# Partial sums seeded into accumulator banks by ScalarE, and the second norm's modulation made wholly by dot products on VectorE

## The chip, the cores and the metric

The kernel runs on one core of a Trainium2 chip. A core has four compute engines, each with its own queue that is worked off in order: TensorE (PE in the profile; its weight loads are a row of their own, PEld), VectorE (DVE), ScalarE (ACT) and GpSimd (POOL). SyncE (SP) issues most DMA transfers. The metric is the device time of one execution in microseconds (us), the median of several runs.

## The reference

One layer of a diffusion backbone runs over two groups of 128 tokens, the prompt (s = 0) and the sample (s = 1), with the same float32 weights and D = 2048. Cut to what matters here:

```python
m = jax.nn.silu(cvec) @ w_ada + b_ada               # per group: shift1, scale1, gate1, shift2, scale2, gate2
h = rms_norm(x, norm1_w) * (1 + sc1) + sh1
p = h @ w_in                                        # q, k, v of two mixers and two gates: 8704 columns
oa, ob = attention of mixer A and of mixer B        # QK-norm, softmax, 8 heads each
y = (sigmoid(ga) * (oa @ w_br_a) + sigmoid(gb) * (ob @ w_br_b)) @ w_out
x = x + g1 * y
h2 = rms_norm(x, norm2_w) * (1 + sc2) + sh2
x = x + g2 * (square(relu(h2 @ w_up)) @ w_down)     # 2048 -> 8192 -> 2048
```

The outputs are both groups' x and the keys and values of the prompt.

## The kernel before, in words

**Steps.** Every weight comes in tiles of 128 x 1024 float32 (512 KB): two blocks of 128 rows by 512 columns. One such tile is a *step*, numbered through the whole kernel (456 of them, the list `wsteps`). For a step the tile is loaded by SP (`add_step`, line 215), ScalarE rounds it to a high part `wH` (`copy`, line 93) and VectorE subtracts to get the low part `wL` (line 241). Then TensorE makes 12 matmuls: two row blocks, two token groups, and three products each (high x high, low weight x high, high x low activation; `mm3`, lines 291 to 293). An accumulator is one bank of 128 x 512 float32; eight banks exist, four in the pool `pacc` for accumulators and four in `paux`.

**The order by hand.** `run` goes through the steps and emits, for each: the loads that are due (lead `LOAD` plus the digit of `RUN`), the splits up to a look-ahead (the digit of `LOOK`), its matmuls, and then whatever was hung on that step with `at`, `ex` or `load_at`. All constants at the top of the file (`LOOK`, `RUN`, `DOTS`, `POST`, `JOBS` and so on) are such places. For the steps in `LO_DMA` the low part is not made on VectorE: ScalarE writes the negated high part (line 247) and a DMA on the POOL queue adds the weight to it (line 248).

**Stages by step.** Steps 0 to 71 are nine units of the first projection (q, k, v), in five chunks of row blocks (`CHUNKS`: 2, 2, 2, 4 and 6, so 1, 1, 1, 2 and 3 steps a unit), because `h` becomes ready block by block. After its chunk a unit's two banks are copied out by ScalarE (first chunk, `first_evac`) or added to what is in SBUF by VectorE (line 400). Steps 72 to 135 are the gates, with the attention among them (`qk_stat`, `qk_apply`, `att_job`); 136 to 167 the two branch projections; 168 to 199 `w_out` and the second norm; then `w_up` and `w_down` in eight pieces of two 512-column blocks. From the second piece on, some tiles of `w_up` go through a Strassen form (`up_pair`, `FAST`): tiles `tH`, `uH`, `YB`, `XL` are made by VectorE and ScalarE, and seven products replace eight. After each piece come four `down_unit`s. Their partial sums over the pieces are kept in SBUF, `dsum`: the first is copied, the others are added by VectorE (line 1257) or copied and then added by a DMA of the POOL queue (`SUM_DMA`, line 1261). `gate_sum` (lines 1238, 1239) multiplies by the gate and adds to x before the last piece, whose units are added by `resid`.

**The modulation.** silu(c) @ w_ada is made in two ways. On TensorE, by column blocks of 128 (`pair_load`, `pair_mm`, line 308: 32 matmuls a block for shift and scale, from four loads of 512 KB), then a copy by ScalarE, transposes on TensorE (`ada_cols`, line 326) and a few small operations on VectorE. Or on VectorE as *dots*: a transposed weight tile of 128 x 1024 (`dot_load`, 512 KB) times the condition row, broadcast to all partitions (`cB`), with the sum taken along the columns (line 1327). One job is one block, one part and one half of the 2048 rows; it needs one dot for each group. The two gates go as dots entirely; of the second norm's 16 blocks the first 6 (`FB_DVE`) go through TensorE, the other 10 as dots; of the first norm's 16 blocks 14 go through TensorE. The condition row is loaded for each of five runs of jobs, and SiLU is applied each time (`silu_cond`, lines 1309, 1310).

Of the kernel before, what the change touches and what calls it, by code (L numbers as in the profile page):

```python
# [10 lines left out]
F32 = mybir.dt.float32  # L11
# [21 lines left out]
FB_DVE = 6  # L33
FB1 = 14
H_AT = 41
DOTS1 = [11, 17, 20, 28, 28, 31, 34, 37]
CHUNKS = [2, 2, 2, 4, 6]
NFAST = 8
FAST = {1: (0, 3, 7), 2: (0, 2, 6, 7), 3: (0, 2, 4, 5, 7), 4: (0, 2, 4, 5, 7), 5: (0, 3, 4, 5, 7), 6: (0, 2, 4, 5, 7), 7: (0, 1, 2, 4, 5, 7)}
SUM_DMA = [5, 6, 11, 13, 16, 19, 21, 23, 25, 27]  # L40
AWAY = [('gA', 1), ('gB', 2), ('gB', 3), ('gA', 0), ('gB', 0), ('gA', 2)]
GATE_BACK = 8
DIRECT = (3,)
LO_DMA = [70, 83, 107, 131, 176, 184, 233, 292, 314, 328, 402, 404]
LO_AHEAD = 2

LOOK = "443323444122344433223333332123333453344534333554455544344534333543324554444555556665556644444333333333332222122312344544555434333333342344333334333323445566643344456656533344434444445455564546555553444554322355444554433333333434334533333333333654544332334455543444555653215536544523333334543233333332223323365455455443222212233432443334434642333334444544534434333333333325434222223333434444444434555642255353443444442222432331122132223342112223332233345544"
RUN = "301110000000010212223333322222222221111122244455544355434445554334554445555664543433234334444445665543321222222212444444444444442222222232223344444455544544444444555455454445566644455555554543365434343355445756644443566664333312222234552332223333334545332333333333322211122222332233322212233323323332332112344444442343322211333343334323233334544422742222212223445554422333233322222211222333333435767545333110221112232111233456655566567556433435335553333334"
CONST_AT = [65, 67]
XL_DMA = []  # L50
ADA_AT = [None, 4, 13, 18, 21, 36, 29]
XS_AT = {1: 13, 2: 18, 3: 29}
POST = {('kvA', 0): [67, 70, 75], ('qA', 0): [70, 73, 78], ('qA', 1): [72, 74, 80], ('kB', 0): [77, 83, 90], ('qB', 0): [82, 84, 93], ('kB', 1): [86, 91, 93], ('qB', 1): [90, 93, 97]}
JOBS = [[79, 80, 80, 87, 93], [81, 83, 88, 90, 93], [87, 87, 89, 90, 99], [93, 93, 96, 99, 102], [96, 97, 100, 105, 112], [102, 103, 107, 112, 123], [105, 107, 111, 118, 123], [112, 115, 118, 121, 123]]
SS_AT = [43, 51, 73, 75, 139, 139]
T_AT = [4, 4]
PREP_IN = [6, 7]
DOTS = [33, 39, 42, 43, 47, 47, 48, 49, 52, 54, 55, 57, 60, 62, 69, 70, 73, 77, 80, 84, 90, 91, 92, 92, 94, 98, 101, 103, 103, 105, 108, 110, 111, 112, 115, 118, 120, 121, 122, 122, 126, 127, 128, 129, 130, 132, 132, 136, 137, 138, 138, 143, 144, 147, 147, 150, 153, 155, 157, 161, 164, 167, 170, 172, 173, 174, 175, 176, 177, 178, 179, 182]
DOTS2 = [230, 232, 234, 235, 236, 237, 240, 243, 255, 263, 265, 269, 270, 288, 301, 301, 307, 328, 328, 331, 333, 334, 358, 360, 361, 363, 366, 368, 391, 391, 395, 399]
STAT_AT = [-1, 0, 10, 16]  # L60
T_PAIR = [[8, 9], [6, 8], [8, 9], [7, 8], [10, 11], [8, 9], [12, 11]]
P_PAIR = [[4, 2], [2, 4], [3, 4], [1, 3], [6, 6], [3, 3], [6, 5]]
M_TE = (3,)
M_AT = [1, 3, 9]
FLIP = 1
P_UP = [4, 1]
# [5 lines left out]
def tile_hybrid_step(ctx: ExitStack, tc: tile.TileContext, a):  # L72
# [13 lines left out]
    def SM(n, name):  # L86
        return sp.tile([P, 32], F32, name=name, tag="s", bufs=14)[:, :n]
# [195 lines left out]
    def mm3(acc, stat, st, first, last, order=(0, 1)):  # L283

        wh, wl = st["hl"]
        for k in range(2):
            kk = 2 * st["half"] + k
            for tb in order:
                sh, sl = stat(kk, tb)
                f, l = first and k == 0, last and k == 1  # L290
                pe.matmul(acc[tb], sh, wh[:, k, :], start=f, stop=False)  # L291
                pe.matmul(acc[tb], sh, wl[:, k, :], start=False, stop=False)  # L292
                pe.matmul(acc[tb], sl, wh[:, k, :], start=False, stop=l)  # L293
# [77 lines left out]

    def first_evac(u, acc):
        units[u] = G(f"u_{u[0]}{u[1]}").rearrange("p (s n) -> p s n", s=2)
        for tb in range(2):
            copy(units[u][:, tb, :], acc[tb])

    def start_steps(u, k0, nk):

        box = {}

        def mm(st, kt):
            if kt == 0:
                box["acc"] = [bank("acc", pacc) for _ in range(2)]
            acc = box["acc"]
            wh, wl = st["hl"]
            last = kt + 2 == nk
            for k in range(2):
                g, kg = divmod(k0 + kt + k, 4)
                for tb in range(2):
                    sh, sl = hH[g][:, kg, tb, :], hL[g][:, kg, tb, :]  # L390
                    pe.matmul(acc[tb], sh, wh[:, k, :], start=kt == 0 and k == 0, stop=False)  # L391
                    pe.matmul(acc[tb], sh, wl[:, k, :], start=False, stop=False)  # L392
                    pe.matmul(acc[tb], sl, wh[:, k, :], start=False, stop=last and k == 1)  # L393
            if not last:
                return
            if k0 == 0:
                first_evac(u, acc)
                return
            for tb in range(2):
                dve.tensor_tensor(units[u][:, tb, :], units[u][:, tb, :], acc[tb], op=OP.add)  # L400
            box.clear()

        for kt in range(0, nk, 2):
# [1094 lines left out]
```

## Time and profile before

| | |
|---|---|
| median of three runs | 1333.61 us |
| the three runs | 1331.23, 1333.61, 1334.71 us |
| span of the profiled execution | 1331.3 us |
| TensorE busy | 1316.0 us, 99% |
| VectorE busy | 1190.2 us, 89% |
| ScalarE busy | 800.8 us, 60% |
| moved by DMA | 392.24 MB, mean 295 GB/s |

The profiled execution has no time of its own beside its span; the three runs lie from 0.1 us below that span to 3.4 us above. "L291" is line 291 of the kernel. In a group line stand the line, the engine, the operation, the tiles written and read, their shapes and the count; after the first bar the busy time of all and the mean of one in ns; after the second the idle time in front of them and what ended it. In a timeline line stand the start and the duration in us and, in brackets, the idle time before and its releaser. In a table by stretches each engine's busy time stands with its number of instructions in brackets. Ends of matmuls are modelled, so starts are what to go by.

### The profile page before, as it was taken

What the parts mean: (1) busy time and instruction counts of PE and PEld (TensorE: products, weight loads), DVE (VectorE), ACT (ScalarE), POOL (GpSimd) and SP (SyncE); (2) the same over time, 40 slices, a digit from 0 to 9 for tenths busy, and PEclk for the clock granted to TensorE, in tenths of its full rate; (3) what the DMA queues carried; (4) which work ended last, traced back from release to release, by engine and by line L of the source; (5) the groups of instructions that cost most, each with busy time, mean ns of one, the idle gap of its engine ahead of it and who ended that gap; (6) DMA issues with size and microseconds to landing.
All of it is one profiled execution on the core that took longest, in us unless ns stands there. A gap on an engine that the chain in (4) does not pass through costs nothing.

```text
span 1331.3 us, 18039 instructions
## 1 busy us (share of the span) xinstructions
PE 1316.0 (99%) x6411; PEld 1067.0 (80%) x6412; DVE 1190.2 (89%) x1546; ACT 800.8 (60%) x979; POOL 54.6 (4%) x64
## 2 busy tenths in 40 slices
PE   8999999999999999999999999999999999999998
PEld 4777778788888878888888888888888888877887
DVE  4699999988898999999779998998999999989685
ACT  5534443476656446635677866758577576676660
POOL 0000000521000000000000000000000000000000
PEclk9999999999999999999999999999999999999999
DMA  9999998986589999996578876988798696878962
GB/s 374 409 409 408 409 401 300 384 277 240 177 329 355 381 392 356 354 367 214 191 230 280 281 254 215 291 273 266 235 296 255 237 301 206 311 195 291 331 213 98
DMA packets 148267, 392.24 MB, mean 295 GB/s; under 512 B 51793, under 2 KB 53009, under 8 KB 148177
## 3 DMA queue, kind: packets, MB, share of 16 engines
q1 hardware_dynamic: 144448, 378.16, 78.8%
q0 software_dynamic: 3584, 12.85, 5.0%
q8 instruction: 50, 0.82, 0.3%
q14 instruction: 41, 0.33, 0.1%
q10 hardware_dynamic: 144, 0.08, 0.0%
HBM read 367.16 MB, written 8.68 MB: 282 GB/s over the span
## 4 chain that ended last, share of the span: by engine, by line
PE 92%; DMA 4%; DVE 2%; ACT 1%; issue 1%; SPq 0%; DVEq 0%; ACTq 0%
PE acc L291 16%; PE acc L292 16%; PE acc L293 16%; PE Q L1117 6%; PE Q L1119 6%; PE Q L1118 6%; PE acc L391 4%; PE acc L392 4%; PE acc L393 4%; DMA araw<-in_w_pair 3%; PE ps_ada L308 2%; PE ps_S L707 1%; PE Z L1119 1%; PE Z L1117 1%; PE Z L1118 1%; DMA aT<-in_w_adaT 1%
## 5 line engine op out<-in xcount | busy, mean ns | idle before, releaser
L241 DVE TENSOR_TENSOR wL<-raw,wH 128x1024 fp32r<-128x1024 f32 x375 | 446.6, 1225 | 72.0 <-ACT wH L93 67.9
L93 ACT ACTIVATE wH<-raw 128x1024 fp32r<-128x1024 f32 (+1 forms) x393 | 392.8, 1044 | 128.3 <-PE acc L392 23.3
L391 PE MATMUL acc<-wH,hH 128*128 128x512 f32 x276 | 109.1, 395 | 0.0
L393 PE MATMUL acc<-wH,hL 128*128 128x512 f32 x276 | 107.5, 390 | 0.0
L392 PE MATMUL acc<-wL,hH 128*128 128x512 f32 x276 | 107.5, 389 | 0.0
L291 PE MATMUL acc<-wH,hH 128*128 128x512 f32 x256 | 101.4, 396 | 0.0
L293 PE MATMUL acc<-wH,hL 128*128 128x512 f32 x256 | 99.7, 390 | 0.0
L292 PE MATMUL acc<-wL,hH 128*128 128x512 f32 x256 | 99.7, 390 | 0.0
L1327 DVE CUSTOM_DVE_ANT_0 aT<-aT,cB,cols 128x1024 f32<-128x1024 f32 x56 | 71.7, 1286 | 0.2
L1327 DVE CUSTOM_DVE_ANT_0 junk<-aT,cB,cols 128x1024 bf16<-128x1024 f32 x56 | 71.4, 1280 | 0.0
L93 ACT ACTIVATE tH<-t 128x1024 fp32r<-128x1024 f32 x33 | 35.0, 1061 | 58.0 <-DVE t L1172 55.4
L391 PEld LDWEIGHTS acc<-wH,hH 128*128 128x128 f32 x276 | 51.8, 188 | 13.6 <-issue 2.5
L393 PEld LDWEIGHTS acc<-wH,hL 128*128 128x128 f32 x276 | 51.8, 188 | 11.0
L392 PEld LDWEIGHTS acc<-wL,hH 128*128 128x128 f32 x276 | 51.8, 188 | 10.4
L293 PEld LDWEIGHTS acc<-wH,hL 128*128 128x128 f32 x256 | 48.0, 188 | 10.2
L291 PEld LDWEIGHTS acc<-wH,hH 128*128 128x128 f32 x256 | 48.1, 188 | 9.8 <-ACT sq L622 0.4
L292 PEld LDWEIGHTS acc<-wL,hH 128*128 128x128 f32 x256 | 48.1, 188 | 9.4
L93 ACT ACTIVATE uH<-raw 128x1024 fp32r<-128x1024 f32 x33 | 35.1, 1063 | 31.6 <-DVE raw L1177 28.6
L1223 ACT ACTIVATE up<-up 128x1024 f32<-128x1024 f32 x28 | 29.7, 1062 | 26.8 <-DVE up L1217 26.3
L308 PE MATMUL ps_ada<-araw,cpad 128*32 128x256 f32 x640 | 39.1, 382 | 2.7 <-DMA araw<-in_w_pair 2.5
L93 ACT ACTIVATE fTa<-pTa 128x2048 uint16<-128x2048 uint16 x16 | 40.5, 2533 | 2.0 <-PE acc L292 1.4
L1172 DVE TENSOR_TENSOR t<-raw 128x1024 f32<-128x1024 f32 x33 | 40.2, 1219 | 1.0 <-PE acc L292 1.0
(641 smaller groups left out, 3316.7 us busy)
## 6 DMA issues: line engine op xcount, KB each, us to landing
raw<-in_w_in SPq DMA_DIRECT2D x133, 512.0 KB, 9.5
raw<-in_w_down SPq DMA_DIRECT2D x128, 512.0 KB, 5.6
araw<-in_w_pair SPq DMA_DIRECT2D x80, 512.0 KB, 10.2
raw<-in_w_upF SPq DMA_DIRECT2D x66, 512.0 KB, 5.2
aT<-in_w_gT SPq DMA_DIRECT2D x64, 512.0 KB, 6.9
raw<-in_w_up SPq DMA_DIRECT2D x62, 512.0 KB, 5.0
aT<-in_w_adaT SPq DMA_DIRECT2D x48, 512.0 KB, 9.6
raw<-in_w_out SPq DMA_DIRECT2D x32, 512.0 KB, 9.6
```

The costliest lines, as they stand in the source:

```text
L93: act.activation(out, in_, AF.Copy)
L241: dve.tensor_tensor(st["lo"], st["raw"], st["hi"].bitcast(F32), op=OP.subtract)
L291: pe.matmul(acc[tb], sh, wh[:, k, :], start=f, stop=False)
L292: pe.matmul(acc[tb], sh, wl[:, k, :], start=False, stop=False)
L293: pe.matmul(acc[tb], sl, wh[:, k, :], start=False, stop=l)
L391: pe.matmul(acc[tb], sh, wh[:, k, :], start=kt == 0 and k == 0, stop=False)
L392: pe.matmul(acc[tb], sh, wl[:, k, :], start=False, stop=False)
L393: pe.matmul(acc[tb], sl, wh[:, k, :], start=False, stop=last and k == 1)
L1117: pe.matmul(acc, stat[0], hi, start=f, stop=False)
L1118: pe.matmul(acc, stat[0], lo, start=False, stop=False)
L1119: pe.matmul(acc, stat[1], hi, start=False, stop=l)
L1327: dve.tensor_tensor_reduce(out, box["raw"], cB[s, tag], 1.0, dst if second else baT[:, part, fb:fb + 1], OP.mult, OP.add, dst)
```

## The change

- `FB_DVE` is 0: all 16 blocks of the second norm's shift and scale are dots (24 jobs more), and no column block of it goes through TensorE any more.
- A dot is a `scalar_tensor_tensor` (times 1.0, times the row) with `accum_out`, where a `tensor_tensor_reduce` stood. It gives a plain sum; the second half of the rows goes to a small tile of its own, and `dot_sum` adds the halves and the bias once.
- SiLU is applied to each half of the condition row once and written to DRAM by the POOL queue; later runs load the result.
- First projection: where `SEED1` has a 1, ScalarE copies the partial sum from SBUF into the two banks (`seed`, two steps ahead), the chunk's matmuls add to it, and ScalarE copies the result out. The last two units of a chunk keep their banks and are the first two of the next (`KEEP`; the order of units alternates). Two unit-chunks keep the addition on VectorE.
- Last stage: the same for `dsum` (`seed` three steps ahead, or at the end of a Strassen pair). The DMA sums, line 1257 and `gate_sum` go; the last piece's banks hold the whole sum.
- `qk_stat` takes its sums of squares on ScalarE, head by head, with `accum_out`; the softmax division becomes four scaled copies on ScalarE.
- `LO_DMA` has 22 steps, where it had 12; 18 of them, where it had 6, lie before step 200. The Strassen tiles of a pair stand at other positions, as many as before. `LOOK`, `RUN` and the other places are set anew.

```diff
-FB_DVE = 6
+FB_DVE = 0
-SUM_DMA = [5, 6, 11, 13, 16, 19, 21, 23, 25, 27]
+SEED_AT = 3
+KEEP = True
+SEED1_AT = 2
+SEED1 = "011111011101111111111110111111111111"
-LO_DMA = [70, 83, 107, 131, 176, 184, 233, 292, 314, 328, 402, 404]
+LO_DMA = [70, 85, 107, 119, 130, 132, 134, 139, 140, 143, 154, 163, 176, 183, 184, 187, 189, 195, 233, 258, 292, 393]
-SS_AT = [43, 51, 73, 75, 139, 139]
+SS_AT = []
...
+        def seed():
+            seeds1[u] = banks()
+            for tb in range(2):
+                copy(seeds1[u][tb], units[u][:, tb, :])
...
-                    pe.matmul(acc[tb], sh, wh[:, k, :], start=kt == 0 and k == 0, stop=False)
+                    pe.matmul(acc[tb], sh, wh[:, k, :], start=opened[u] and k == 0, stop=False, skip_group_check=skip)
...
+        if seeded:
+            at(i - SEED1_AT, seed)
...
+    turned = first_units[7:] + first_units[2:7] + first_units[:2]
...
         for s in range(2):
-            act.activation(sq[:, s].rearrange("p h d -> p (h d)"), raw[:, s, 0:nh * HD], AF.Square)
-        ssq, r = SM(2 * nh, "ssq"), SM(2 * nh, "rq")
-        dve.tensor_reduce(ssq.rearrange("p (s h) -> p s h", s=2), sq, axis=AX.X, op=OP.add)
+            for h in range(nh):
+                act.activation(sq[:, s, h, :], raw[:, s, h * HD:h * HD + HD], AF.Square,
+                               accum_out=ssq[:, s * nh + h:s * nh + h + 1])
...
-            dve.tensor_tensor(prob[:, :, 0:nk], prob[:, :, 0:nk], rd.unsqueeze(2).to_broadcast([P, 4, nk]), op=OP.mult)
+            for h in range(4):
+                act.activation(prob[:, h, 0:nk], prob[:, h, 0:nk], AF.Copy, scale=rd[:, h:h + 1])
...
+    def seed(p, n):
+
+        seeds[p, n] = [bank("acc", pacc) for _ in range(2)]
         for s in range(2):
-            dve.tensor_tensor(d[:, s, :], d[:, s, :], gbc["g2", n][:, s, :], op=OP.mult)
-            dve.tensor_tensor(x1[n][:, s, :], x1[n][:, s, :], d[:, s, :], op=OP.add)
+            copy(seeds[p, n][s], dsum[n][:, s, :])
...
             for s in range(2):
-                if p == last:
-                    out_s(acc, n, s)
-                elif p == 0 or by_pool:
-                    copy(part[:, s, :], acc[s])
-                else:
-                    dve.tensor_tensor(dsum[n][:, s, :], dsum[n][:, s, :], acc[s], op=OP.add)
...
-                pool.dma_start(dsum[n], part, accum_op=OP.add)
+                copy(dsum[n][:, s, :], acc[s])
...
+        if p and (n or p == last):
+            at(len(wsteps) - SEED_AT, lambda: seed(p, n))
...
-    def silu_cond(s, tag):
+    def silu_cond(h, s, tag):
+        if (s, h) in silu_row:
+            return
         t, c = G("sgB"), cB[s, tag]
         act.activation(t, c, AF.Sigmoid)
         dve.tensor_tensor(c, c, t, op=OP.mult)
+        silu_row[s, h] = dp.tile([1, 1024], F32, name=f"silu{s}{h}")
+        pool.dma_start(silu_row[s, h], c[0:1, :])
...
-        dve.tensor_tensor_reduce(out, box["raw"], cB[s, tag], 1.0, dst if second else baT[:, part, fb:fb + 1],
-                                 OP.mult, OP.add, dst)
+        dve.scalar_tensor_tensor(out, box["raw"], 1.0, cB[s, tag], op0=OP.mult, op1=OP.mult,
+                                 accum_out=dst[:, s, fb:fb + 1])
+
+    def dot_sum(dst, which, part, f0=0):
+        n = KC - f0
+        dve.tensor_tensor(dst, dst, half2.pop(which)[:, :, f0:KC], op=OP.add)
+        dve.tensor_tensor(dst, dst, baT[:, part, f0:KC].unsqueeze(1).to_broadcast([P, 2, n]), op=OP.add)
```

214 lines of the change are left out of this document (127 added, 87 removed).

## The prediction

> **What bounds the kernel now.** First the page: busy time, the slices, the chain that ended last.
>
> ```profile
> PE 1316.0 (99%) x6411; PEld 1067.0 (80%) x6412; DVE 1190.2 (89%) x1546; ACT 800.8 (60%) x979; POOL 54.6 (4%) x64
> ...
> PE   8999999999999999999999999999999999999998
> ...
> DVE  4699999988898999999779998998999999989685
> ACT  5534443476656446635677866758577576676660
> ...
> DMA  9999998986589999996578876988798696878962
> ...
> PE 92%; DMA 4%; DVE 2%; ACT 1%; issue 1%; SPq 0%; DVEq 0%; ACTq 0%
> ```
>
> TensorE is busy in every slice and holds 92% of the chain; VectorE (DVE) stands at 8 or 9 tenths beside it, ScalarE (ACT) at 3 to 7. A busy TensorE row can hide gaps, so next the timeline of a quiet stretch, to see whether matmuls really follow each other:
>
> ```profile
> 599.72 0.39 PE L291 MATMUL acc<-wH,m0H 128*128 128x512 f32 x1
> ...
> 602.44 0.39 PE L291 MATMUL acc<-wH,m0H 128*128 128x512 f32 x1
> ```
>
> Between these two lie 12 matmuls, one weight step: 2.72 us a step, 0.227 a matmul. The change leaves the number of 512-column matmuls as it is (the Strassen positions move, but their number, 33, stays), so time can go only where TensorE does other work or waits. The last place to look is the one long wait in the later half, in the timeline and the table by stretches (columns: TensorE, weight load, VectorE, ScalarE, GpSimd, clock, DMA share, GB/s):
>
> ```profile
> 1195.58 0.39 PE L1119 MATMUL Q<-YB,h20L 128*128 128x512 f32 x1
> 1199.57 0.80 PE L1117 MATMUL Q<-tH,sH 128*128 128x512 f32 x1 [3.60 <-ACT dsum L93]
> ```
> ```profile
> 1195.00:1205.00 10.00, 6.40 (x22) 4.87 (x21) 9.86 (x12) 6.04 (x8) 0.87 (x1) 0.83 0.91 270
> ```
>
> TensorE stood 3.6 us at the head of the last Strassen pair and then ran at a granted clock of 0.83 over the ten us: about 5.3 us lost in all (3.6, and 0.17 of the 10). VectorE was busy 9.86 of these 10: it was late, not idle.
>
> **The change, part by part. (1) The modulation as dots.** FB_DVE goes from 6 to 0, so the six column blocks that TensorE made for the second norm (line 308) go, with their three gathers and transposes (line 326). From the chain in order of time, and the timeline:
>
> ```profile
> 170.45 1.86 PE ps_ada L308 x32
> 194.30 1.86 PE ps_ada L308 x32
> 256.72 1.86 PE ps_ada L308 x32
> 264.25 1.86 PE ps_ada L308 x32
> ...
> 473.50 3.59 PE ps_ada L308 x64
> ```
> ```profile
> 103.61 0.60 PE L326 MATMUL ps_sel<-ident,S 128*128 128x128 f32 x4
> ```
>
> 4 x 1.86 + 3.59 = 11.0 us, and 3 x 0.60 = 1.8 for transposes: **12.8 us off TensorE**, all of it on the path. In exchange 6 blocks x 2 parts x 2 halves = 24 jobs, each one 512 KB load on SP's queue (for 24 such loads that go: bytes equal) and two dots: 48 dots more, and all 272 dots (224 before) take another instruction.
>
> ```profile
> L1327 DVE CUSTOM_DVE_ANT_0 aT<-aT,cB,cols 128x1024 f32<-128x1024 f32 x56 | 71.7, 1286 | 0.2
> L1327 DVE DVE_READ_ACCUMULATOR2_ANT gc_g<- 128x1 f32 x128 | 10.8, 84 | 0.0
> ```
> ```profile
> L1333 DVE SCALAR_TENSOR_TENSOR scT<-scT,cols x2: 159/167/175, 168.2 to 610.2; 128x4 f32<-128x4 f32 x1, 128x20 f32<-128x20 f32 x1
> ```
>
> A dot costs 1.28 + 0.08 = 1.37 us now. The new instruction does not run here at this size with a sum. The nearest rows are the old dot (same operands, same sum) and line 1333, the same instruction on two SBUF operands: 159 ns for 4 elements, 175 for 20, so 1.0 ns an element over a fixed 155. By that 1024 elements take 155 + 1024 = 1.18 us, 1.26 with the read of the sum; at two cycles an element 155 + 2048 = 2.20, with the read 2.28. I take 1.30, between line 1333's price and the old dot, and keep 1.26 and 2.28 as ends. The Trainium skill (Vector Engine (DVE) Microarchitecture Reference, section Points that are easy to get wrong) says that this instruction with two non-bf16 SBUF sources halves throughput, with no port left for the accumulator. Line 1333 disagrees for the form without a sum; no run here shows the form with one. By that rule the time is that of the third rival below.
>
> **(2) Sums in the banks.** In the first projection 72 additions on VectorE (line 400) become 4; in the last stage 28 (line 1257) and the 16 of gate_sum (1238, 1239) become none. Each goes to ScalarE as a copy into the bank before the unit's matmuls and one out of it after.
>
> ```profile
> L241 DVE TENSOR_TENSOR wL<-raw,wH 128x1024 fp32r<-128x1024 f32 x375 | 446.6, 1225 | 72.0 <-ACT wH L93 67.9 <-DMA aT<-in_w_gT 3.2 <-issue 0.5
> ...
> L1257 DVE TENSOR_TENSOR dsum<-dsum,acc 128x512 f32<-128x512 f32 x28 | 18.2, 683 | 2.7 <-PE acc L293 2.7
> ...
> L1310 DVE TENSOR_TENSOR cB<-cB,sgB 128x1024 f32<-128x1024 f32 x10 | 12.1, 1220 | 1.0 <-DMA raw<-in_w_in 1.0
> ...
> L624 DVE TENSOR_REDUCE ssq<-sq 128x8 f32<-128x1024 f32 x6 | 7.3, 1214 | 0.0
> ...
> L746 DVE TENSOR_TENSOR prob<-prob,rd 128x1024 f32<-128x1024 f32 x4 | 4.9, 1226 | 0.1
> ...
> L746 DVE TENSOR_TENSOR prob<-prob,rd 128x512 f32<-128x512 f32 x4 | 2.8, 693 | 0.1
> ```
> ```profile
> sum 588.90, DVE 46.44; mean DVE 4.22
> ```
> ```profile
> L93 ACT ACTIVATE wH<-raw 128x1024 fp32r<-128x1024 f32 x387 | 389.4, 1051 | 128.3 <-PE acc L392 23.3 <-DMA raw<-in_w_in 21.7 <-PE acc L293 19.4
> ...
> L93 ACT ACTIVATE dsum<-acc 128x512 f32<-128x512 f32 x28 | 16.0, 594 | 24.3 <-PE acc L293 22.5 <-PE acc L292 1.2
> ...
> L732 ACT ACTIVATE prob<-ps_S,nm 128x128 f32<-128x128 f32 x16 | 5.7, 367 | 10.5 <-DVE nm L730 7.7 <-DVE nm L728 2.7
> ...
> L732 ACT ACTIVATION_READ_ACCUMULATOR prob<-ps_S,nm 128x1 f32 x24 | 4.9, 203 | 0.0
> ```
>
> The row that begins "sum 588.90" is line 400 alone, over 53 to 642 us. No copy into a bank is in the trace; the nearest is the copy out, 0.594; I take that and do not expect it far off either way.
>
> **(3) The rest.** qk_stat and the softmax division move from VectorE to ScalarE, the SiLU of the condition is made 4 times rather than 10, and 22 weight parts rather than 12 come by an accumulating DMA: each spares VectorE one line-241 subtraction (1.225) for a ScalarE copy near the price of a wH copy (1.05) and a POOL DMA. 18 of the 22 lie before the second norm (6 before).
>
> **VectorE up to 642 us,** against the stretches:
>
> ```profile
> 53.10:81.90 28.80, 28.80 (x178) 22.57 (x177) 27.41 (x40) 12.40 (x16) 0.00 (x0) 1.00 1.03 409
> 81.90:115.00 33.10, 33.10 (x246) 24.86 (x245) 30.67 (x51) 14.84 (x19) 0.00 (x0) 1.00 1.03 409
> ...
> 446.10:505.00 58.90, 58.90 (x311) 47.38 (x311) 57.52 (x82) 26.87 (x30) 0.00 (x0) 1.00 1.03 385
> 505.00:553.90 48.90, 48.90 (x217) 40.52 (x216) 48.72 (x62) 34.78 (x31) 0.00 (x0) 1.00 1.01 351
> 553.90:598.40 44.50, 44.50 (x202) 36.90 (x202) 43.83 (x61) 19.18 (x24) 1.73 (x2) 1.00 1.02 378
> ...
> sum 588.90, PE 588.65 PEld 477.98 DVE 552.40 ACT 310.23 POOL 37.83; mean PE 53.51 PEld 43.45 DVE 50.22 ACT 28.20 POOL 3.44
> ```
>
> Off: 68/72 of 46.4 = 43.9; reductions 8.0; divisions 7.7; 12 subtractions 14.7; 2 SiLU products 2.4; together 76.7. On: 208 dots at 1.30 less 160 at 1.37 = 51. So 552.4 - 76.7 + 51 = 527, where TensorE now needs 588.9 - 12.8 = 576. VectorE gets freer, not tighter. Behind 642 us it loses another 18.2, 16 x 0.683 = 11 for gate_sum at line 1257's price, and 4 x 1.22 = 5 of SiLU.
>
> **ScalarE** takes up 26 seeds x 2 and 52 more copies out in the first projection (62 us), 84 copies in the last stage (50), some 35 us in the attention (52 squares at 0.37 + 0.20 less 14 at about 0.6, 32 divisions at about 0.43) and 10 DMA copies: about 155, so 955 of 1318, which has room on the whole. It has little in the second and third chunk of the projection (steps 9 to 26, the first two stretches above): a seeded step asks for 4 x 0.594 + 1.05 = 3.43 us where TensorE takes 2.72, and the seed must follow the copy out of the step two earlier, whose banks it takes. Over the chunks it comes to 12.4 + 24 x 0.594 = 26.7 of 28.8 us, and 14.8 + 28 x 0.594 = 31.4 of 33.1. Bounds: nothing, if the look-ahead covers it; 11 steps x 0.71 = 8 us, if nothing does. I take 2.5. Behind a late seed in ScalarE's queue stand the wH copies, and VectorE's subtractions behind those. In the last stage a seed has three steps (8 us) for 1.2 us of copies; I cost it at nothing. At the head of a pair's down stage it has the last 18 matmuls (4.1 us); the cover is gone if VectorE's additions run late.
>
> **The 5.3 us at 1195.** On VectorE ahead of it:
>
> ```profile
> 1177.84 0.08 DVE L1327 DVE_READ_ACCUMULATOR2_ANT gc_g<- 128x1 f32 x1
> ...
> 1186.81 1.28 DVE L1257 TENSOR_TENSOR dsum<-dsum,acc 128x512 f32<-128x512 f32 x2
> ```
>
> The pair's tiles lose two dsum additions (1.3 us) in front of them, and the last dots, which end here at 1178, move three steps earlier; but the joins that hold VectorE too are placed anew. I take 3.5 of the 5.3.
>
> Sum on the profiled execution: 1331.3 - 12.8 - 3.5 + 2.5 + 0.5 for small waits = 1318.0. Its span lies at the low end of the three times shown (1331.23, 1333.61, 1334.71), 2.3 below their median; with that, **1320 us**, 1.0% faster. A change under 0.3% (4 us) would not be told from none in this kernel.
>
> **Rivals.** *ScalarE becomes the bound in steps 9 to 26.* For it: the 93 to 95% just worked out, in an engine that waits on two others. Against it: those chunks hold TensorE work of another kind (3.6 us per pair of column blocks) that gives it time. With the full 8 us and as much again in late wH copies, and nothing won at 1195: 1320 + 3.5 + 8 + 0.5 = 1332, no change.
>
> *Transfers become the bound from step 110 to 184.* Slower than before. For it: DMA share 1.01 to 1.03 at 351 to 385 GB/s in the three stretches from 446 us. That part of the code asks for 12 more dot loads and 9 more accumulating loads, and 8 pair loads fewer: 13 x 0.52 MB = 6.8 MB, 18 us at 380 GB/s. Against it: TensorE waits for none there now, and earlier loads and the look-ahead (about 4 steps, 11 us) can hide most. Unhidden it gives 1320 + 18 = 1338; it decides from 10 us unhidden.
>
> *VectorE at half rate per dot.* At 2.28 us, 208 dots cost 474 rather than 270, VectorE needs 731 us where TensorE needs 576: 1320 + 155 = 1475. It passes TensorE from (576 - 552.4 + 76.7 + 219) / 208 = 1.54 us a dot on. Against it: line 1333's slope and the old dot. This is the case that the skill's rule names.
>
> **Chances.** The forecast, from 1309 (all waits gone) to 1328: 0.70. ScalarE, 1332: 0.12, a quarter of it still under 1329.6. Transfers, 1338: 0.11. Half rate, 1475: 0.07. Faster 0.73, same 0.09, slower 0.18. The range 1309 to 1346 leaves out the half rate and a little at each end.
>
> **What would show it.** Line 308 with 448 matmuls instead of 640, and TensorE's rows still 0.227 apart. The dot's row at 1.18 to 1.29 us; above 1.5 the forecast is wrong. Line 400 with 4 rows, VectorE's busy time near 1120 to 1150, ScalarE's near 950. In 53 to 115 us, waits of matmuls for ScalarE's bank copies: under 3 us right, over 8 the first rival. From step 110 on, waits for loads in front of wH copies that reach TensorE: the second. At the head of the last pair, a wait under 2 us.

## The result, and the profile after

The changed kernel takes **1356.28 us** (median; 1354.82 to 1359.45), against 1333.57 for the kernel before beside it: a ratio of 1.0176, 95% interval 1.0163 to 1.0188. It is 1.8% slower, 36 us above the forecast and 10 us above the range. The profiled execution has a span of 1354.1 us.

From the page after: busy time, the slices, two of the queues, the chain.

```profile
PE 1314.1 (97%) x6208; PEld 1064.8 (79%) x6208; DVE 1131.8 (84%) x1499; ACT 915.7 (68%) x1290; POOL 55.7 (4%) x68
...
PE   8999999999999896998999999999999999999998
...
DVE  4557899988898986989788998997998999979655
...
PEclk9999999999999997998999999999999999999999
DMA  9999998887699999999668976778677595857583
...
q1 hardware_dynamic: 144448, 378.16, 78.1%
q0 software_dynamic: 3712, 12.86, 5.0%
...
PE 49%; DVE 3%; ACT 1%; issue 1%; DMA 1%; DVEq 0%; ACTq 0%
```

VectorE's total is as forecast (1131.8, forecast 1120 to 1150). TensorE's is not: 1316.0 less 12.8 us of work would be 1303, and it is 1314.1. So of the 36 us above the forecast some 11 are matmuls that took longer, and 25 are idle time (40.0 us of the span, 15.3 before). TensorE has slices at 6 and 8 tenths, between about 440 and 640 us, and the granted clock dips there. The next groups below answer the single terms: line 313 is the old line 308, line 1383 the dot.

```profile
L413 PE MATMUL acc<-wH,hH 128*128 128x512 f32 x276 | 108.8, 394 | 0.3 <-ACT acc L98 0.3
...
L313 PE MATMUL ps_ada<-araw,cpad 128*32 128x256 f32 x448 | 27.5, 382 | 2.7 <-DMA araw<-in_w_pair 2.5
```
```profile
L1383 DVE SCALAR_TENSOR_TENSOR junk<-aT,cB 128x1024 bf16<-128x1024 f32 x136 | 164.4, 1229 | 0.0
L1383 DVE SCALAR_TENSOR_TENSOR aT<-aT,cB 128x1024 f32<-128x1024 f32 x136 | 164.0, 1225 | 0.5
```

448 matmuls instead of 640, as forecast; TensorE's first matmuls in the first projection waited 0.3 us in all for ScalarE's bank copies; and the new dot costs 1.23 us, as much as the plain product of that size in the kernel before (line 1310, 1.22).

So where do 22.7 us come from? The next table counts, from the first matmul of the kernel, when TensorE begins a step, and gives each kernel's difference to the kernel before. The columns behind "after" are experiments of the next section. The profiled execution of `a_fb6` took 1363.53 us, 6 above that kernel's median.

| step | before, us | after | a_lo_few | a_fb6 | c_fb6 | d_fb0 | d_fb6_ns |
|---|---|---|---|---|---|---|---|
| 27 | 113.8 | +0.8 | +0.7 | +1.1 | +0.6 | +0.6 | +0.6 |
| 78 | 271.3 | -7.6 | -7.7 | +2.5 | +4.2 | -4.8 | +0.7 |
| 120 | 412.4 | -7.3 | -7.2 | +2.1 | +3.8 | -5.2 | +0.3 |
| 138 | 466.7 | +4.5 | +5.8 | +2.6 | +4.3 | -1.9 | +0.8 |
| 141 | 479.1 | +0.4 | +1.7 | +15.0 | +4.3 | -6.0 | +0.8 |
| 153 | 512.0 | +1.7 | +9.0 | +14.9 | +4.2 | -4.5 | +0.7 |
| 156 | 520.1 | +15.4 | +9.0 | +33.8 | +4.3 | -2.7 | +0.8 |
| 180 | 586.3 | +16.0 | +9.0 | +33.8 | +4.3 | +14.5 | +0.8 |
| 184 | 597.2 | +25.6 | +16.3 | +33.8 | +6.1 | +18.2 | +2.6 |
| 199 | 639.7 | +25.6 | +18.2 | +34.4 | +6.1 | +18.6 | +2.6 |
| last matmul | 1325.1 | +22.7 | +15.4 | +30.4 | +2.6 | +15.4 | -0.8 |

Up to step 120 the changed kernel is 7 us ahead, as forecast. Then it loses 33 us up to step 199: 12 between 120 and 138, 14 at once between 153 and 156, 10 between 180 and 184. Behind that it wins 2.9: at the last Strassen pair, where TensorE stood 3.6 us before, it now waits 0.5. What TensorE and ScalarE waited for in the changed kernel from 400 to 660 us (total, times, longest):

```profile
ACT wH L98 <- DMA raw<-in_w_br_b: 25.1, 5, 16.1
ACT wH L98 <- DMA raw<-in_w_out: 21.1, 7, 6.4
...
ACT wH L98 <- DMA raw<-in_w_br_a: 17.4, 4, 9.1
...
PE acc L297 <- DMA wL<-in_w_br_a: 11.1, 1, 11.1
...
PE acc L297 <- DVE wL L246: 8.8, 5, 3.7
```

Two things are late: transfers (three rows of loads, and the 11.1 us for one low part that came by an accumulating DMA) and VectorE (five low parts). The long wait in the timeline, with what stood on SP's and POOL's queues ahead of it:

```profile
501.74 11.17 SPq L867 DMA_TRANSPOSE pTm<-plm  x1
```
```profile
505.41 0.86 POOL L253 DMA_DIRECT2D wL<-in_w_br_a  x1 [31.59 <-ACT wL L252]
```
```profile
529.06 0.79 PE L297 MATMUL acc<-wL,oHA 128*128 128x512 f32 x1 [11.11 <-DMA wL<-in_w_br_a]
529.65 0.63 PE L298 MATMUL acc<-wH,oLA 128*128 128x512 f32 x1
530.08 0.63 PE L296 MATMUL acc<-wH,oHA 128*128 128x512 f32 x1
```

The accumulating DMA of step 154 was issued at 505.4, into a DMA transpose that held SP's queue for 11.2 us, and its data came so late that TensorE stood until 529.1. Between 515 and 525 us the DMA engines were busy throughout (a mean share of 1.31 to 1.35) and moved 58 to 76 GB/s. The next matmuls start 0.43 us apart instead of 0.23: the granted clock had fallen during the wait, to 0.50 to 0.52 between 520 and 530 us.

The tables by stretches, 50 to 250, 250 to 420 and 420 to 640 us (columns as in the prediction), first before, then after:

```profile
50.00:250.00 200.00, 199.75 (x1175) 156.99 (x1174) 192.75 (x286) 86.83 (x105) 13.09 (x12) 1.00 0.99 386
250.00:420.00 170.00, 170.00 (x891) 140.09 (x890) 148.42 (x218) 105.66 (x205) 21.33 (x19) 1.00 0.78 278
420.00:640.00 220.00, 220.00 (x1050) 181.70 (x1049) 211.94 (x284) 118.91 (x136) 3.41 (x5) 1.00 0.94 337
```
```profile
50.00:250.00 200.00, 198.74 (x1121) 157.57 (x1120) 166.63 (x250) 142.03 (x231) 17.07 (x19) 1.00 0.98 381
250.00:420.00 170.00, 168.29 (x839) 139.31 (x837) 146.81 (x223) 122.46 (x307) 19.45 (x17) 1.00 0.82 295
420.00:640.00 220.00, 196.44 (x836) 159.71 (x835) 195.38 (x285) 114.10 (x121) 12.04 (x14) 0.93 1.05 335
```

The reader should see where the relief on VectorE fell: 26 us in the first stretch, where TensorE was busy throughout already. In the last stretch VectorE had 8 us of 220 to spare before, and transfers stood at 0.94; after, transfers stand at 1.05 and VectorE idles 25 us while TensorE loses 24.

### The profile page after: what moved, and what is told of

Read it like the earlier page. It is cut to its first block, busy times and chain, and to the rows that moved or that the text cites. A ratio compares the mean times of both kernels' runs of the same rounds, so it can differ in the third digit from the quotient of the medians.

```text
span 1354.1 us, 17872 instructions
## 1 busy us (share of the span) xinstructions
PE 1314.1 (97%) x6208; PEld 1064.8 (79%) x6208; DVE 1131.8 (84%) x1499; ACT 915.7 (68%) x1290; POOL 55.7 (4%) x68
## 3 DMA queue, kind: packets, MB, share of 16 engines
q1 hardware_dynamic: 144448, 378.16, 78.1%
q0 software_dynamic: 3712, 12.86, 5.0%
## 4 chain that ended last, share of the span: by engine, by line
PE 49%; DVE 3%; ACT 1%; issue 1%; DMA 1%; DVEq 0%; ACTq 0%
PE acc L297 9%; PE acc L298 9%; PE acc L296 9%; PE Q L1160 5%; PE Q L1161 5%; PE Q L1159 5%; DMA wL<-in_w_up 1%; PE Z L1161 1%; PE Z L1160 1%; PE Z L1159 1%; DVE wL L246 1%; PE acc L981 1%; PE acc L998 1%; PE acc L979 1%; PE acc L996 1%
## 5 line engine op out<-in xcount | busy, mean ns | idle before, releaser
L246 DVE TENSOR_TENSOR wL<-raw,wH 128x1024 fp32r<-128x1024 f32 x365 | 434.1, 1223 | 130.7 <-ACT wH L98 125.5
L1383 DVE SCALAR_TENSOR_TENSOR junk<-aT,cB 128x1024 bf16<-128x1024 f32 x136 | 164.4, 1229 | 0.0
L1383 DVE SCALAR_TENSOR_TENSOR aT<-aT,cB 128x1024 f32<-128x1024 f32 x136 | 164.0, 1225 | 0.5
L1224 DVE TENSOR_TENSOR uL<-raw,uH 128x1024 fp32r<-128x1024 f32 x33 | 40.4, 1225 | 1.6
L297 PE MATMUL acc<-wL,oHA 128*128 128x512 f32 x64 | 26.8, 419 | 14.8 <-DMA wL<-in_w_br_a 11.1
## 6 DMA issues: line engine op xcount, KB each, us to landing
raw<-in_w_in SPq DMA_DIRECT2D x133, 512.0 KB, 8.7
raw<-in_w_down SPq DMA_DIRECT2D x128, 512.0 KB, 5.4
aT<-in_w_adaT SPq DMA_DIRECT2D x72, 512.0 KB, 9.6
raw<-in_w_upF SPq DMA_DIRECT2D x66, 512.0 KB, 5.0
aT<-in_w_gT SPq DMA_DIRECT2D x64, 512.0 KB, 7.3
raw<-in_w_up SPq DMA_DIRECT2D x62, 512.0 KB, 5.6
araw<-in_w_pair SPq DMA_DIRECT2D x56, 512.0 KB, 10.2
raw<-in_w_out SPq DMA_DIRECT2D x32, 512.0 KB, 11.0
```

The lines of the kernel that those rows point to most:

```text
L246: dve.tensor_tensor(st["lo"], st["raw"], st["hi"].bitcast(F32), op=OP.subtract)
L297: pe.matmul(acc[tb], sh, wl[:, k, :], start=False, stop=False, skip_group_check=seeded)
L1383: dve.scalar_tensor_tensor(out, box["raw"], 1.0, cB[s, tag], op0=OP.mult, op1=OP.mult, accum_out=dst[:, s, fb:fb + 1])
```

## The experiments

Theories at the start. **A:** the stretch from step 120 to 190 has two full resources, VectorE and transfers; the dots overfill the one and the accumulating parts put in their place overfill the other. **B:** one collision (step 154's accumulating DMA beside a DMA transpose) is the bulk. **C:** the ScalarE copies, or the new look-ahead and lead digits, do the harm.

### The accumulating parts

`a_lo_few` is the kernel after with ten accumulating parts rather than 22:

```diff
-LO_DMA = [70, 85, 107, 119, 130, 132, 134, 139, 140, 143, 154, 163, 176, 183, 184, 187, 189, 195, 233, 258, 292, 393]
+LO_DMA = [70, 85, 107, 131, 176, 184, 233, 258, 292, 393]
```

> The changed kernel with LO_DMA of steps 119 to 195 cut from 15 to 3 (131, 176 and 184 stay as before the change), so 12 low parts go back to VectorE (12 x 1.22 = 15 us). If the accumulating transfers are what overloads the stage from step 119 to 195, the 27 us that TensorE loses there mostly return: 1322 to 1335 us. If the 12 more loads of dots are the cause, transfers fall short all the same and VectorE has more to do: 1348 to 1360. If it is one collision of a DMA transpose with the accumulating transfer of step 154, that one goes with the rest: about 17 us less, 1336 to 1342.

`a_no154` takes only step 154 out of that list; `a_mat` leaves the list and moves the DMA transposes of the branch projections:

```diff
-M_AT = [2, 5, 9]
+M_AT = [1, 3, 9]
```

> The changed kernel with step 154 alone taken out of LO_DMA, the one whose low part TensorE waits 11.3 us for while a DMA transpose runs. Collision as the cause of most of the loss: the wait and the half clock behind it go, 1337 to 1343 us. A stage overloaded by all accumulating transfers: one of 15 goes, 1350 to 1355, with waits turning up a few steps later. Loads of dots as the cause: no change, 1354 to 1358.

> The changed kernel with the DMA transposes of the merged branches issued after 1 and 3 steps as before the change (M_AT 1, 3, 9) in place of 2 and 5, away from the accumulating transfer of step 154. Collision: the wait at 517 us shrinks by half or more, 1338 to 1350 us. Overload by accumulating transfers or by dot loads: 1352 to 1360, since the same bytes move in the same stage.

`b_lo_many` is the kernel before with the changed kernel's 18 places before step 200:

```diff
-LO_DMA = [70, 83, 107, 131, 176, 184, 233, 292, 314, 328, 402, 404]
+LO_DMA = [70, 85, 107, 119, 130, 132, 134, 139, 140, 143, 154, 163, 176, 183, 184, 187, 189, 195, 233, 292, 314, 328, 402, 404]
```

> The kernel before with the 12 accumulating transfers more that the change puts at steps 119 to 195, and nothing else of the change. If they overload the stage by themselves: 1345 to 1360 us, with waits of wH copies for loads between 420 and 640 us. If it takes the dot loads too, VectorE is freed of 15 us and nothing is lost: 1329 to 1336.

Measured: `a_lo_few` 1350.59 (1.0131, 1.0113 to 1.0148), `a_no154` 1344.10 (1.0085, 1.0068 to 1.0101), `a_mat` 1348.72 (1.0115, 1.0100 to 1.0130), `b_lo_many` 1350.21 (1.0129, 1.0114 to 1.0144). The stretch 500 to 550 us of `a_no154`, where the changed kernel had its long wait:

```profile
500.00:550.00 50.00, 49.21 (x217) 40.43 (x217) 49.22 (x67) 30.95 (x29) 0.86 (x1) 1.00 1.07 346
```

Taking away either partner of the collision, the accumulating DMA or the transpose's place, takes the 11 us wait away: B names a real part, worth 12 us by the first (1356.28 to 1344.10) and 8 by the second (to 1348.72). That is half of the loss against the kernel before and a third of what the forecast missed: 11 us of loss stay (1332.68 for the kernel before beside it), and the gain that was forecast is missing. The eleven other parts do no harm here on the whole: `a_no154` has eleven more than `a_lo_few` and is 6.5 us faster. In `a_lo_few` no load reaches TensorE any more, but another resource stands at its limit:

```profile
420.00:640.00 220.00, 203.64 (x877) 165.70 (x878) 214.27 (x308) 105.56 (x112) 2.58 (x3) 0.97 0.92 328
```
```profile
PE acc L297 <- DVE wL L246: 12.7, 6, 4.1
PE ps_gr L1404 <- DVE gc_g L1389: 3.3, 1, 3.3
```

VectorE is busy 214 of 220 us, and between 400 and 660 us TensorE waits 16 us for it. In `b_lo_many`, which has no dot more, it is the transfers: the loads of the two column blocks at step 139 come late.

```profile
PE ps_ada L308 <- DMA araw<-in_w_pair: 5.7, 8, 1.5
```
```profile
450.00:500.00 50.00, 44.28 (x220) 31.51 (x219) 32.02 (x47) 17.87 (x20) 2.59 (x3) 0.86 1.04 375
```

Here 5.7 us of waits cost 11.6 from step 138 to 141, as the clock fell with them: it was 0.50 from 480 to 490 us, the pair's groups of eight matmuls took 1.08 us instead of 0.64, and the nine wide ones behind came 0.43 apart. The parts cost 17 us in all, in a kernel where they also spare VectorE twelve subtractions.

### The two halves of the change apart

`a_fb6_few` undoes the dots part and the accumulating parts and keeps the rest; `a_fb6` undoes only the dots part; `a_fb6_lr` adds the old digits of `LOOK` and `RUN` for steps 90 to 199 to `a_fb6_few`; `b_fb0` is the kernel before with all blocks as dots, at the changed kernel's places. The edit of `a_fb6`:

```diff
-FB_DVE = 0
+FB_DVE = 6
-SS_AT = []
+SS_AT = [43, 51, 73, 75, 139, 139]
-DOTS = [33, 40, 40, 42, 43, 43, 47, 47, 47, 50, 52, 52, 55, 57, 57, 57, 58, 62, 62, 67, 70, 70, 73, 75, 82, 84, 84, 88, 90, 92, 92, 93, 95, 96, 99, 99, 99, 103, 103, 105, 108, 108, 108, 111, 112, 114, 114, 118, 119, 120, 121, 121, 124, 124, 124, 125, 125, 126, 128, 129, 130, 130, 132, 132, 134, 136, 136, 138, 140, 143, 143, 144, 149, 151, 151, 152, 153, 157, 157, 157, 166, 169, 169, 170, 173, 174, 175, 175, 175, 176, 177, 179, 179, 182, 182, 183]
+DOTS = [33, 39, 42, 43, 47, 47, 48, 49, 52, 54, 55, 57, 60, 62, 69, 70, 73, 77, 80, 84, 90, 91, 92, 92, 94, 98, 101, 103, 103, 105, 108, 110, 111, 112, 115, 118, 120, 121, 122, 122, 126, 127, 128, 129, 130, 132, 132, 136, 137, 138, 138, 143, 144, 147, 147, 150, 153, 155, 157, 161, 164, 167, 170, 172, 173, 174, 175, 176, 177, 178, 179, 182]
```

> The kernel after with the six column blocks of the second norm on TensorE again and ten accumulating weight parts, four of them between steps 107 and 184; what stays of the change are the sums in the banks, the moved squares and divisions and the new dot instruction. Theory one (the second norm's extra dots, their loads and the accumulating transfers put in to pay for them overfill steps 120 to 190): TensorE takes back 12.8 us of work, the loss of 33 us from step 114 to 190 goes, the 3.6 us won at the last pair stay: 1333.5 - 3.6 = 1330, between 1327 and 1334, VectorE under 0.97 in 440 to 660 us and no wait of TensorE over 2 us there. Theory two (the sums on ScalarE delay the rounding of the weights, or the new look-ahead digits hurt by themselves): waits for wH or loads stay in that stretch, 1340 or more.

> The same as the kernel before it in this list, but with all 22 accumulating parts, eighteen of them before step 200. If accumulating transfers alone overfill the transfers, as the 17 us say that the same places cost in the kernel before the change: 1330 + 10 to 17 = 1340 to 1347, with waits of TensorE or ScalarE for loads between 440 and 640 us. If they hurt only together with the extra dots' loads: within 3 us of the kernel before it in this list.

> As the first of this list, with the look-ahead and lead digits of the kernel before for steps 90 to 199. If the new digits are part of the loss: 3 us or more under the first of this list. If not: within 2 us of it, or slower.

> The kernel before with the six blocks as dots, at the places that the kernel after has for them, with the old dot instruction and six accumulating parts before step 200. Theory one, VectorE's half of it: 48 dots at 1.37 are 66 us more on an engine that had 552 of 589 us busy up to 642 us, so 618 us of VectorE work where TensorE needs 576: about 29 us over the old 589, 1333.5 + 29 = 1362, at least 1350, with VectorE at 1.00 from 440 us on. If only the transfers are short: the loads that it shifts into that stage are 12, 6.3 MB or 16 us at 380 GB/s, 1333.5 - 12.8 + 16 = 1337.

Measured: `a_fb6_few` 1340.57 (1.0054, 1.0039 to 1.0069), `a_fb6` 1357.41 (1.0189, 1.0165 to 1.0212), `a_fb6_lr` 1339.48 (1.0047, 1.0032 to 1.0061), `b_fb0` 1389.15 (1.0418, 1.0402 to 1.0433).

The digits for steps 90 to 199 are worth 1 us, with overlapping intervals: that half of C falls there. With many accumulating parts the kernel is as slow without the extra dots (1357.4) as with them (1356.3); the parts cost 16.8 us there, with waits of TensorE between 400 and 660 us for the loads of the pair at step 139 and for the gate's column sums, which stood in VectorE's queue behind low parts whose weights were late:

```profile
ACT wH L98 <- DMA raw<-in_w_br_b: 28.2, 7, 17.1
...
PE ps_gr L1404 <- DVE gc_g L1389: 16.9, 1, 16.9
PE ps_ada L313 <- DMA araw<-in_w_pair: 6.7, 8, 2.3
```

In this profiled execution, 6 us slower than the median, the pair at step 139 lost 12 us, as in `b_lo_many`, and steps 153 to 156 lost 19, where `a_fb6_few` lost 7. The second place is step 154 again: its accumulating DMA was issued at 518.3, into a DMA transpose that held SP's queue for 10.8 us from 514.6, and between 525 and 530 us 47 GB/s moved at a DMA share of 1.34. No run takes that one part out of `a_fb6`. So the two equal times are made of different losses: the changed kernel has no pair at step 139.

`b_fb0` was expected at 1362 and took 1389. Its first and last stretch:

```profile
50.00:250.00 200.00, 190.82 (x1071) 148.91 (x1070) 193.58 (x291) 82.95 (x98) 7.71 (x8) 0.99 0.95 364
...
420.00:640.00 220.00, 199.09 (x860) 161.79 (x858) 208.45 (x285) 110.00 (x123) 2.60 (x3) 0.94 0.90 329
```

Without the relief TensorE waits in the first stretch too. So the sums and the other moves are worth something to the dots: `a_lo_few`, with the same number of dots, is 39 us faster (that includes the cheaper dot instruction, 1.23 against 1.29 us and a read of 0.08; the parts were not separated).

`a_fb6_few` missed its 1330 by 10 us. Its one long wait is the same row as above, `ps_gr` for `gc_g`, 5.4 us: the transpose of the gate's rows stands behind an in-order VectorE queue. The next run takes that away.

### How many dots fit, and where

In the kernel before 16, 20 and 36 dot jobs lie before step 73, from 73 to 119, and from 120 on; in the changed one 22, 27 and 47. A job is two dots, 2.46 us. The following kernels all have ten accumulating parts and one edit more, which emits the sum of the gate's halves on VectorE eight steps ahead of the transpose:

```diff
-    i = ROWS_AT[0] + max(i for i, (job, h, n) in placed if job[0] == "g1")
+    i = 2 + max(i for i, (job, h, n) in placed if job[0] == "g1")
+    ex(i, lambda: dot_sum(gcol["g1"], "g1", 2))
+    i = ROWS_AT[0] - 2 + i
```

`c_fb6` is `a_fb6_few` with that edit. `c_fb4`, `c_fb2` and `c_fb0` have `FB_DVE` 4, 2 and 0, the first 22 jobs as in the changed kernel, and the others spread evenly: 30, 33 and 36 from step 73 to 118, 28, 33 and 38 from 120 to 182.

> The first of the previous list (six column blocks on TensorE, ten accumulating parts; 1340.6), with one edit: the sum of the gate's halves is emitted on VectorE two steps after the last gate dot, and the transpose on TensorE stays eight steps behind it. Its only TensorE wait over 1.1 us behind 300 us was the 5.4 us in front of that transpose, with the slower clock after it. If that is the whole loss beyond the early 2.5 us: 1340.6 - 7 = 1333.5, between 1331 and 1336, so the sums in the banks alone are worth nothing. If the wait only moves: above 1338.

> The kernel after with four column blocks on TensorE, ten accumulating parts, the gate's sum as in the one before, and the dots spread evenly: thirty of them from step 73 to 118, twenty-eight from 120 to 182. Theory one (VectorE has room for a part of the extra dots, mostly between 240 and 420 us): one pair of blocks off TensorE, 1333.5 - 4 = 1329, between 1326 and 1333. Theory two (VectorE is full already with 72 dot jobs): 1338 or more, with waits for wL between 440 and 640 us.

> The same with two column blocks on TensorE and thirty-three dots in each of the two stretches. Theory one with room for sixteen jobs of 2.46 us: 1333.5 - 8 = 1325. If room ends at about eight to ten jobs: 1330 to 1336, waits for wL come back.

> The same with none, thirty-six dots from 73 to 118 and thirty-eight from 120 to 182. The kernel after with ten accumulating parts took 1350.6, with about 23 us of waits and slow clock between steps 120 and 184 as VectorE was full. Moving eight to nine jobs of 2.46 us forward out of that stretch should take 15 to 21 us off: 1330 to 1336. If VectorE is full from step 73 on, no more than 5 us go: 1345 or more.

Measured: `c_fb6` 1334.73 (1.0012, 1.0003 to 1.0021), `c_fb4` 1353.57 (1.0151, 1.0134 to 1.0168), `c_fb2` 1353.27 (1.0147, 1.0132 to 1.0162), `c_fb0` 1363.54 (1.0221, 1.0205 to 1.0237).

`c_fb6` came as expected: the sums part alone leaves the time where it was. Its first and last stretch:

```profile
50.00:250.00 200.00, 197.57 (x1156) 154.65 (x1156) 149.97 (x221) 136.38 (x211) 11.76 (x16) 0.99 0.97 376
...
420.00:640.00 220.00, 218.50 (x1044) 180.19 (x1043) 204.00 (x283) 119.83 (x135) 2.59 (x3) 1.00 0.95 342
```

The whole of it frees 43 us of VectorE in the first stretch and 8 in the last. The evenly spread kernels missed by 24 us and more, for a reason that none of the theories had. From `c_fb4`, TensorE's row from 250 to 400 us, and VectorE's timeline ahead of that wait's end:

```profile
PE ps_PT L792 <- ACT prob L785: 7.3, 1, 7.3
```
```profile
324.37 1.22 DVE L1383 SCALAR_TENSOR_TENSOR aT<-aT,cB 128x1024 f32<-128x1024 f32 x1
...
325.51 1.22 DVE L1383 SCALAR_TENSOR_TENSOR junk<-aT,cB 128x1024 bf16<-128x1024 f32 x1
...
326.66 0.68 DVE L764 TENSOR_REDUCE mx<-ps_S 128x4 f32<-128x512 f32 x1
...
327.66 1.22 DVE L1383 SCALAR_TENSOR_TENSOR aT<-aT,cB 128x1024 f32<-128x1024 f32 x1
...
328.99 0.18 DVE L783 RECIPROCAL rd<-den 128x4 f32<-128x4 f32 x1
```

Dots stand in front of the row maxima and the reciprocals of the softmax, each 1.2 us, and ScalarE's scaled copies and TensorE's transposes of `prob` wait behind them. From 250 to 420 us the changed kernel has VectorE busy 147 of 170 us, 86%, and `c_fb4` 137 of 170: the waits come while VectorE has idle time, and what counts there is how soon a short operation gets its turn. Three jobs too many and the wrong places are not separated, since `c_fb4` differs from the changed kernel in both; `d_fb4` below, with the changed kernel's places there, loses 0.1 us from step 78 to 120. From step 120 to 126 `c_fb4` loses another 4 us in the last of the attention; from there to step 184, with most of its 28 late jobs, it goes from +26.8 to +23.4, and these 3.4 us are nearly the pair of column blocks that it lacks at step 139: almost no loss.

The last six put that together: the first 49 jobs as in the changed kernel, then 31 (`d_fb4`) or 47 (`d_fb0`) evenly from step 120 to 182; `d_fb6_ns` and `d_fb4_ns` are `c_fb6` and `d_fb4` without seeds in the first projection:

```diff
-SEED1 = "011111011101111111111110111111111111"
+SEED1 = "000000000000000000000000000000000000"
```

> The kernel after with four column blocks on TensorE, ten accumulating parts, the gate's sum emitted early, its own 49 dots up to step 119 and 31 dots evenly from step 120 to 182. If VectorE holds about 30 dots there and the loss of the evenly spread kernel came from its dots in front of the softmax alone: no wait over 2 us from 260 to 640 us, and 1334.7 less one pair of blocks, 3.7 to 4.3 us: 1330, between 1327 and 1333. If 31 are too many: 1335 or more with waits for wL.

> The same with no column block on TensorE: 47 dots evenly from step 120 to 182. These are 16 dot jobs more than in the kernel before it in this list, 39 us of VectorE on a stretch that has about 3: 30 us or more of waits for wL and gate rows between 412 and 640 us against 8.6 us of TensorE work less: 1330 + 30 - 9 = 1351, between 1345 and 1358. If the loss of the kernel after were due to the bunched places of its dots and not to their number: under 1340.

> The kernel with six column blocks on TensorE, ten accumulating parts and the early gate sum (1334.7), without seeds in the first projection: 52 additions on VectorE where 104 copies on ScalarE were. If the 43 us that the seeds free on VectorE between 50 and 250 us are not used, because transfers are full there and nothing can be moved in: the 2 to 4 us of early waits for ScalarE's bank copies go and it takes 1330 to 1334. If they are needed by the dots of that stretch: waits for wL before 260 us, 1338 or more.

> The first of this list without seeds in the first projection. If the seeds' room is not used: within 3 us of the first of this list. It has 22 dots before step 73 where the one with six blocks has 16, so if it is used it is here: 5 us or more slower, with waits for wL before 260 us.

Measured: `d_fb4` 1336.73 (1.0024, 1.0014 to 1.0033), `d_fb0` 1348.67 (1.0110, 1.0095 to 1.0125), `d_fb6_ns` 1332.34 (0.9996, 0.9986 to 1.0006), `d_fb4_ns` 1338.15 (1.0033, 1.0021 to 1.0044). From `d_fb0` and from `d_fb6_ns`:

```profile
420.00:640.00 220.00, 202.93 (x874) 164.09 (x873) 217.44 (x310) 107.08 (x115) 2.59 (x3) 0.97 0.94 332
```
```profile
50.00:250.00 200.00, 199.77 (x1175) 157.00 (x1174) 179.39 (x273) 88.02 (x116) 13.98 (x16) 1.00 0.97 380
```

With all 47 jobs late VectorE is busy 217 of 220 us and the kernel loses 24 us between steps 120 and 199, at other places than `a_lo_few` (25.4 lost) but as much: number, not bunching. Against `c_fb6`, which differs in the dots part alone, it is 14 us slower. And without the seeds VectorE carries 29 us more in the first stretch, and with 72 dot jobs TensorE is busy 199.77 of these 200 us all the same: the seeds' room is hardly used. With 80 jobs it is worth 1.4 us, with overlapping intervals. The copies have a price of their own: in `c_fb6` TensorE waited 2.4 us for them between 50 and 260 us and lost 3.5 from step 36 to 52, and nothing there in `d_fb6_ns`, which is 2.4 us faster (again with slightly overlapping intervals). `d_fb4`, expected at 1330, took 1336.73: one pair of blocks fewer on TensorE (4.2 us) is paid for with waits, 3.6 us from step 120 to 132 and 2.3 from 168 to 174.

Two more, with 80 jobs, stem from `d_fb4`: `e_fb4a` moves the blocks that stay on TensorE to steps 73, 75 and 139, and `e_fb4b` then spares three subtractions and moves two jobs from the late stretch to between steps 72 and 118:

```diff
-SS_AT = [43, 51, 73, 75]
+SS_AT = [73, 75, 139, 139]
```
```diff
-LO_DMA = [70, 85, 107, 131, 176, 184, 233, 258, 292, 393]
+LO_DMA = [70, 79, 85, 91, 98, 107, 131, 176, 184, 233, 258, 292, 393]
```

> The kernel with four column blocks on TensorE and 31 dots from step 120 (1336.7), with the two pairs of blocks at steps 73, 75 and 139 in place of 43, 51 and 73, 75. TensorE's work is the same; up to step 60 it should be 3.7 us plus the early waits ahead (the kernel after stood at -4.4 there), and the pair at step 139 gives VectorE 4.3 us of cover in its full stretch. If VectorE's room there is what counts: 1328 to 1332. If the early gain is only moved: 1334 to 1338, within 3 us of the one it stems from.

> The same with accumulating weight parts at steps 79, 91 and 98 too, two dots moved forward from the late stretch (29 left there). If VectorE's late stretch is still what binds: 2 to 5 us under the one before. If the moved dots stand in front of the softmax: 3 us or more over it, with waits of TensorE for prob between 300 and 330 us.

Measured: `e_fb4a` 1337.82 (1.0037, 1.0024 to 1.0049), `e_fb4b` 1345.12 (1.0096, 1.0081 to 1.0112). The first is no better: the early gain is only moved. The second loses 9 us between steps 78 and 102, by waits of TensorE for the softmax's `prob` and for `T_qA`, as its other branch had it. No version here beats the kernel before.

## Why the prediction was wrong

**Right:** the work off TensorE (448 matmuls at line 313; 4.5 us won between steps 36 and 52, 4.5 between 73 and 78 and 4.1 between 138 and 141 are its pairs of blocks, at 3.7 for the column blocks and 0.6 for the transposes). The dot: 1.23 us and 0.08 for the read, against 1.30 taken and 1.26 and 2.28 as ends. The sentence of the Trainium skill on halved throughput (Vector Engine (DVE) Microarchitecture Reference, section Points that are easy to get wrong) does not hold for this form, with its sum: 1.2 ns an element. The third rival falls with it. ScalarE in steps 9 to 26: 0.6 us lost up to step 27 and 0.3 us of waits, where 2.5 were taken; the first rival falls, and for the changed kernel the half of theory C that blamed the copies (in `c_fb6` they cost some 2 to 4 us, later than step 26). ScalarE's total is 916, some 40 below the sum. The last pair: its wait is gone, and 2.9 us are won behind step 199, where 3.5 were taken.

**Wrong: "VectorE gets freer, not tighter."** 527 of 576 us is a mean over the stretch from 53 to 642, and as a sum it came true. But the step needs it by stretches. The seeds free VectorE up to 250 us; the new jobs go 6, 7 and 11 to the three parts, and the 11 late ones are 27 us. From 420 to 640 us VectorE had 8 us to spare and the moves give it 8 more (204.00 in `c_fb6`), while TensorE gets 4 us shorter: short by some 15, and 24 to 25 us of TensorE with the waits and clock, as `d_fb0` and `a_lo_few` show, with VectorE at 217 and 214 of 220 us and transfers at 0.94 and 0.92. So the dots part, which the forecast had winning 12.8 us, costs 14 with ten accumulating parts (`c_fb6` 1334.73, `d_fb0` 1348.67). The rows that said so stood in the prediction itself: VectorE 57.52 of 58.90, 48.72 of 48.90, 43.83 of 44.50.

Nor do the rows show a good place for the jobs: before 200 us transfers stand at 1.00 to 1.03 (each job brings a load), and between the two the softmax needs VectorE at short notice. No run put more jobs before step 73, so the first half of that is argued.

**Wrong: the accumulating parts, costed as a ScalarE copy and a DMA, with no wait.** Twelve of them at these places cost 17 us in the kernel before, 11.6 of it at the late loads of one pair of blocks. In the page after, queue q0 takes 5.0% of the span for 12.86 MB and q1 78.1% for 378.16, so 1.9 times as long a byte. In the changed kernel twelve cost 6 net (`a_lo_few`), and this is a sum of two: step 154, beside the DMA transpose, costs 12, and the other eleven win 6.5 (`a_no154`), as there they also relieve VectorE.

**The second rival** had the place right, steps 110 to 184, and the sign. Its price, 18 us, and its chance were too low, because it counted bytes alone and took VectorE for free. Of the 33 us lost from step 120 to 199, 14 are the collision at step 154. The two other losses are nearly the same with eleven accumulating parts and without them: 12 us in `a_no154` and 13 in `a_lo_few` from step 120 to 138, 9 and 7 from 180 to 184. TensorE waits there for VectorE in both, and with the parts ScalarE also waits for loads (17.6 us for `in_w_out` between 590 and 625 us in the changed kernel). By these waits the relief of VectorE is paid in transfers at these two places; no run separates the two.

Open: why the transpose of step 154's neighbour and the accumulating DMA slow each other so much (the transpose held the queue for 11.2 us, against 8.7 in `a_no154`, and the accumulating DMA landed after 23.6 us, where the median of its kind is 8.7); only that the wait goes when either is taken away is shown. Also not separated is what each of the moves other than the seeds is worth.

## What to carry to other kernels

Balance an engine by the stretch in which the new work must run, not over a long span: relief that falls elsewhere does not help it. Where an engine and the transfers are both near 95%, moving work between them is no free trade: here eleven parts won 6.5 us, the twelfth lost 12, and the same places cost the kernel before 17. Try each resource's relief by itself first, and look for single collisions before blaming the mean load. In a stretch with a short dependent chain, such as a softmax, a mean load of 85% on an in-order queue can already be too much for long operations at the wrong places.

## What was not expected of the hardware

A `scalar_tensor_tensor` on two float32 operands from SBUF with a column sum runs 1024 elements in 1.23 us, the same as a plain product (1.22). An accumulating DMA issued beside a DMA transpose held TensorE for 11.1 us, while the mean busy share of the DMA engines over these 50 us was 1.13 at 247 GB/s:

```profile
500.00:550.00 50.00, 38.89 (x162) 31.65 (x161) 35.16 (x47) 22.87 (x22) 1.73 (x2) 0.86 1.13 247
```

Without it the same stretch moved 346 GB/s at 1.07. And short waits can cost double their length: in `b_lo_many` eight, of 1.5 us at most and 5.7 in all, took 11.6 us, as the clock fell to 0.50 among them; the one of 11.1 us in the changed kernel took 13.7.
